# W_out's attention rows split ahead of time, mixed pairs kept on chip, v asked for later: one block of a streaming encoder in float32

## The chip, the cores and the metric

The kernel runs on one NeuronCore of a Trainium2 chip. The core has a matrix engine (TensorE, PE in the profile; its weight loads are listed apart as PEld), a vector engine (VectorE, DVE), a scalar engine (ScalarE, ACT), a general engine (GpSimd, POOL) and SyncE (SP), which here only issues DMAs. Each engine works through its own instructions in order and waits on semaphores for the others. The metric is the device time of one execution in microseconds, the median of several runs.

## The reference

One layer of a hybrid block on x of 1024 tokens by 1024 channels, all in float32. FFN width is 4096; the mixer has 8 attention heads of width 64 (512 columns, "FoX") and 512 columns of a gated linear recurrence (RG-LRU).

```python
x = layer_norm(alpha * x + 0.5 * swiglu(x, ffn1_gate, ffn1_up, ffn1_down))
z = x @ w_in                                   # q, k, v, lru x, lru gate, forget gates
fox = forgetting_attention(q, k, v, fg)        # causal softmax(q k / 8 + cum[t] - cum[s]) v
u = causal_depthwise_conv(z_lx, conv_w, conv_b)
lru = gelu(z_lg) * rg_lru(u, ...)
mix = concatenate([fox, lru], axis=-1) @ w_out
x = layer_norm(alpha * x + mix)
x = layer_norm(alpha * x + 0.5 * swiglu(x, ffn2_gate, ffn2_up, ffn2_down))
```

The first 512 rows of `w_out` meet the attention heads; they are its attention rows.

## The kernel before

**Split products.** Every float32 operand is split in two: `hi`, a rounded copy made by ScalarE (`nc.scalar.copy` into a tile of type float32r), and `lo`, the rest, made by VectorE as `x - hi`. A product is three matmuls, hi*hi + hi*lo + lo*hi (`mm3`, lines 166 to 168). A split therefore costs one ScalarE and one VectorE instruction for each tile. The big products use a scheme with seven block products in place of eight (operands "11", "21", "t1" to "t4", "22").

**Stages, in order of time.** Gate/up 1 (0 to about 640 us), down-projection 1 (to about 900), the projections of the mixer with the recurrence (`mixer_in`, to 1163), attention with W_out and the second layer norm (`attention`, 1163 to about 1380), gate/up 2 (to about 1990), down-projection 2.

**Preparation in gate/up 1.** While gate/up 1 runs on TensorE, a generator `prepare` (line 266) splits weights of later stages. Each of its steps takes a 128x256 piece of a weight that SyncE has fetched into an `aux` tile (4 buffers) and hands it to `keep` (line 280): ScalarE casts (L283), VectorE subtracts (L284), GpSimd issues a store of hi and lo to DRAM (L285). The tiles are of the pool that gate/up's own split weights use (15 buffers). `advance` (line 707) takes one step after each of the first six products of either matrix of pairs 1 to 15; what is left is done after gate/up. The jobs are, in order, the v columns of w_in (`wv_d`), the units of q, k and the recurrence (`wq_d`) and the first pair of FFN 2's gate and up (`pre_d`).

**Attention.** 64 units, one for each head h and query tile i of 128 tokens, from i = 7 down to 0; heads 6 and 7 are interleaved. `probs` makes the scores (L1389, L1390), adds the decay, and takes the maximum and the exponential (VectorE L1395, ScalarE L1396). Three units later (two from head 4 on) `to_pT` transposes the probabilities on TensorE (L1410) and splits them while evicting them (ScalarE L1414, VectorE L1415). One unit after that, for every second tile, `values` multiplies with v (L1431); for the odd head of a pair it then splits the pair's columns of the mixed result into `mixes[h // 2]` (L1443, L1444).

TensorE's gaps are filled by `piece`: the 16 products of the recurrence's mixed rows with W_out, spread over units 1 to 35. From unit 36 on there are none left. When the second head of the last pair finishes query tiles, `out_tile` multiplies all four mixed pairs with W_out's attention rows `w_fox` and adds the layer norm; the last output tiles run after the last unit, among the transposes for gate/up 2.

**W_out's attention rows.** At unit 36 `out_w` loads four row tiles of 128x1024 as two raw tiles (L1357); at units 39, 41, 43 and 45 `split_ws` splits one of them (ScalarE L158, VectorE L159).

**Where the mixed pairs live.** Pool `mixp` has two buffers. Pairs 0 and 1 are written there, stored to DRAM by GpSimd (`mix_d`, L1447) and read back by SyncE into `row` buffers at units 40 and 50 (L1532). Pair 2 is in a buffer `w2` of pool `hp`, pair 3 again in `mixp`.

**SyncE's queue.** Loads of a head (`load`, called at i = 5 of the head before, or at unit (6, 6) for head 7) bring q, kh, kl, cum (L1064, L1059) and, in the same call, v (L1374), which has two buffers. `issue_after(x)` puts what is issued inside the block behind x on its own engine's queue, with no semaphore. The rows of x for the residual (`open_row`, L1473) are in the same chain.

**Into gate/up 2.** `ready_pair` fetches the prepared weights of FFN 2's first pair from `pre_d` (L588): "11", "21" and "t1" into `ws` tiles, "t4" and "t2" into two `raw` tiles, later "t3" and "22". These fetches stand behind `mix_load`, the last read-back. The `raw` pool has two buffers for the whole kernel: in attention they hold, in turn, the last q/k unit, the fourth split row of W_out's recurrence rows (until the last `piece`), the two raw tiles of `out_w`, and then "t4" and "t2".

Of the kernel before, what the change touches and what calls it, by code (L numbers as in the profile page):

```python
# [9 lines left out]
F32 = mybir.dt.float32  # L10
F32R = mybir.dt.float32r
# [6 lines left out]
P = 128  # L18
D = 1024
T = 1024  # L20
# [28 lines left out]
def f32(ap):  # L49
    return ap.bitcast(F32)  # L50
# [12 lines left out]
class Block:  # L63
# [274 lines left out]
    def mixer_jobs(self, w_in):  # L338

        view = w_in.rearrange("(k p) f -> p k f", p=P)  # L340
        self.wq_d = self.dram.tile([len(UNITS), len(UNIT_ORDER), P, 2, 2, 2 * P], F32, name="wq_d")
        self.wv_d = self.dram.tile([2, KT, P, 2, 2 * P], F32, name="wv_d")
        jobs = []
        for cc in range(2):
            for k in range(KT):
                c = V_OFF + 256 * cc
                jobs.append(([view[:, k:k + 1, c:c + 256]], self.wv_d[cc, k]))
        for u, cols in enumerate(UNITS):
            jobs += self.quarter_jobs(view, cols, lambda n, h: self.wq_d[u, UNIT_ORDER.index(n)][:, :, h])
        return jobs  # L350
# [15 lines left out]
    def gate_up(self, wg, wu, h_d, rows, bank, tp, wsp, raws=None, later=None, aside=None, ready=None, steps=None):  # L366
# [211 lines left out]
        def ready_pair(g, u):  # L578
# [13 lines left out]
            with self.tc.issue_after(self.mix_load.ins):  # L592
                for n in ("11", "21", "t1"):
                    for m in both:
                        fetch(n, m, two_blocks())
                for n in ("t4", "t2"):
                    r = self.rawp.tile([P, 4, 4, P], F32R, tag="raw", name=self.nm("raw"))
                    for i, m in enumerate(both):
                        fetch(n, m, (r[:, 2 * i], r[:, 2 * i + 1]))
# [751 lines left out]
    def out_w(self, w_out):  # L1351

        raws = []
        for c in range(2):
            raws.append(self.raw([P, 2, D]))
            with self.tc.issue_after(self.row_load.ins):
                self.row_load = self.nc.sync.dma_start(raws[c], w_out[2 * c * P:(2 * c + 2) * P, :].rearrange("(f p) d -> p f d", p=P))  # L1357
        return [r[:, j:j + 1, :] for r in raws for j in range(2)]

    def attention(self, w_out, mixp, ln, x1_d, normed):  # L1360
# [4 lines left out]
        with self.pool("att_t", 1) as tp, self.pool("att_p", 3) as pp, self.pool("att_pt", 6) as ptp, self.pool("att_v", 2, side="right") as vtp:  # L1365

            def load(h):
                b, names = h % 2, ("q", "kh", "kl", "cum")
                if h:
                    with self.tc.issue_after(self.row_load.ins):  # L1370
                        for n in names:
                            self.load_head(h, n)
                vt = vtp.tile([P, NT, P], F32R, tag="v", name=self.nm("v"))
                self.row_load = nc.sync.dma_start(f32(vt), self.v_d[h].rearrange("(j p) d -> p j d", p=P))  # L1374
                q, kh, kl, cum = (self.heads[n][:, b, :] for n in names)
                return q, kh, kl, vt, cum
# [3 lines left out]
            def probs(h, i):  # L1380

                q, kh, kl, _, cum = heads[h]
# [39 lines left out]
            def values(h, qt):  # L1422
                vt = heads[h][3]
# [12 lines left out]
                if b:  # L1436
# [8 lines left out]
                    if qt == 0 and h < 5:  # L1445
                        for l in range(2):
                            nc.gpsimd.dma_start(mix_d[h // 2][l], f32(mixes[h // 2][l]))  # L1447

            heads, pts, ps, outs, mixes = {}, {}, {}, {}, {}
            mix_d = [self.dram.tile([2, P, T], F32, name=f"mix{c}_d") for c in range(2)]  # L1450
# [3 lines left out]
            tiles, mix, w_fox = [], [], []  # L1454
            MIXES = 40, 50
# [21 lines left out]
            with self.tc.issue_after(self.row_load.ins):  # L1477
                heads[0] = load(0)
            open_row(0)
# [6 lines left out]
            def out_tile():  # L1486
                i, d = tiles.pop(0)
                self.down_tile(i, list(zip(mix + [mixes[2], mixes[3]], w_fox)), (d,))
                if d:
                    self.layer_norm(i)  # L1490
                    normed(i)

            for n in range(len(units) + AHEAD + 1):
                if n < len(units):
                    h, i = units[n]
                    if i == 5 and h < 6 or (h, i) == (6, 6):
                        heads[h + 1] = load(h + 1)
                    if i == NT - 1:
                        if h % 2 == 0:
                            outs[h // 2] = tp.tile([P, T], F32, tag="o", name=self.nm("o"))  # L1500
                        else:
                            if h == 5:
                                t = self.hp.tile([P, 2, T], F32R, tag="w2", name=self.nm("mix"))
                                mixes[2] = t[:, 0, :], t[:, 1, :]
                            else:
                                mixes[h // 2] = tuple(mixp.tile([P, T], F32R, tag="h", name=self.nm("mix")) for _ in range(2))
# [15 lines left out]
                if n == 36:  # L1522
                    w_raws = self.out_w(w_out)
                if 39 <= n < 47 and n % 2:
                    w_fox.append(tuple(t[:, 0, :] for t in self.split_ws(w_raws[len(w_fox)], 1)))
# [3 lines left out]
                if n in MIXES:  # L1529
                    mix.append(tuple(self.rowp.tile([P, T], F32R, tag="row", name=self.nm("mix")) for _ in range(2)))  # L1530
                    for l in range(2):
                        self.mix_load = nc.sync.dma_start(f32(mix[-1][l]), mix_d[len(mix) - 1][l])  # L1532
# [6 lines left out]
def kernel(  # L1539
# [15 lines left out]
    with blk.pool("xl", side="right") as xl, blk.pool("x1") as x1, blk.pool("gu_t", 4) as tp, blk.pool("x22") as x22, \  # L1555
# [23 lines left out]
        jobs = blk.mixer_jobs(w_in[0])  # L1579
# [110 lines left out]
```

## Time and profile before

| | us |
|---|---|
| median of 3 runs | 2314.07 |
| range of the runs | 2312.58 to 2314.19 |
| the profiled execution's own time | 2308.6 |
| its span, first to last instruction | 2306.8 |
| mean granted TensorE clock | 0.998 of full speed |

The profile is of one execution. Its page lists busy time by engine, and views of its trace list busy time by stretch of time, groups of instructions by source line, who waited for whom, the chain of waits that ended last, and each engine's instructions in order. A line such as `L1415 DVE TENSOR_TENSOR pt<-a,pt` is read: line 1415, VectorE, the operation, writes tile pt from tiles a and pt. `PE a L1431 <- ACT pt L1414` means that TensorE, about to write tile a on line 1431, waited for ScalarE's writing of pt on line 1414.

### The profile page before, as it was taken

The numbers are of one execution on the slowest core, as the hardware profiler recorded it, in microseconds if no ns is written. First come the engines' busy times: TensorE is split into PE (matmuls) and PEld (weight loads), VectorE is DVE, ScalarE is ACT, GpSimd is POOL, SyncE is SP. The second block draws the span as 40 slices with busy tenths as digits, with TensorE's granted clock in tenths as the row PEclk, the third lists the DMA queues.
The fourth block names the chain that finished last, engine by engine and source line by source line (L and its number), as shares of the span: only waits on it lengthen the run. The fifth ranks groups of instructions, "written<-read, shape, count | busy, mean of one in ns | idle before, by whom it ended". The sixth has DMA issues, their size and how long they took to land.

```text
span 2306.8 us, 29448 instructions
## 1 busy us (share of the span) xinstructions
PE 2278.0 (99%) x10609; PEld 1895.0 (82%) x10609; DVE 1701.5 (74%) x2749; ACT 1063.6 (46%) x1771; POOL 308.4 (13%) x503
## 2 busy tenths in 40 slices
PE   9999999999999999999999999999999999999998
PEld 7878888888888888987788788888888888888887
DVE  8878787878467788877767899665656666577886
ACT  5454545454344335455556755333333343344341
POOL 0242323232000001121133200000000000000000
PEclk9999999999999999999999999999999999999999
DMA  4565656565376444366786734232323232564542
GB/s 155 194 212 210 211 207 216 200 223 188 108 271 221 148 142 149 131 205 203 263 249 165 246 119 151 87 119 87 119 87 119 87 119 87 201 251 159 185 144 73
DMA packets 210321, 387.10 MB, mean 168 GB/s; under 512 B 13616, under 2 KB 112240, under 8 KB 210176
## 3 DMA queue, kind: packets, MB, share of 16 engines
q1 hardware_dynamic: 173760, 262.21, 34.8%
q0 software_dynamic: 36416, 123.02, 13.6%
q8 instruction: 83, 1.36, 0.2%
q14 instruction: 62, 0.51, 0.1%
HBM read 258.27 MB, written 126.91 MB: 167 GB/s over the span
## 4 chain that ended last, share of the span: by engine, by line
PE 87%; DVE 4%; issue 4%; DMA 1%; ACT 1%; POOL 1%; SPq 0%; DVEq 0%; POOLq 0%; ACTq 0%
PE x L166 9%; PE x L168 9%; PE x L167 9%; PE b L166 7%; PE b L167 7%; PE b L168 7%; PE a L168 6%; PE a L166 6%; PE a L167 6%; PE s L168 5%; PE s L167 5%; PE s L166 5%; PE a L1431 1%; PE a L1410 1%; PE a L1093 1%
## 5 line engine op out<-in xcount | busy, mean ns | idle before, releaser
L381 ACT CAST ws<-t 128x512 fp32r<-128x512 f32 x240 | 147.7, 623 | 320.4 <-PE b L167 137.8
L382 DVE TENSOR_TENSOR ws<-t,ws 128x512 fp32r<-128x512 f32 x240 | 163.5, 685 | 71.3 <-ACT ws L381 36.2
L167 PE MATMUL a<-ws,ws 128*128 128x512 f32 x512 | 199.8, 390 | 0.6 <-DVE ws L813 0.6
L166 PE MATMUL b<-As,ws 128*128 128x512 f32 x512 | 199.7, 390 | 0.6 <-ACT As L417 0.4
L166 PE MATMUL a<-ws,ws 128*128 128x512 f32 x512 | 199.3, 390 | 0.4 <-ACT row L705 0.4
L167 PE MATMUL b<-As,ws 128*128 128x512 f32 x512 | 199.5, 390 | 0.0
L168 PE MATMUL a<-ws,ws 128*128 128x512 f32 x512 | 199.4, 390 | 0.0
L168 PE MATMUL b<-As,ws 128*128 128x512 f32 x512 | 199.3, 389 | 0.0
L166 PE MATMUL x<-As,ws 128*128 128x512 f32 x504 | 196.5, 390 | 2.8 <-ACT row L686 1.6
L168 PE MATMUL x<-As,ws 128*128 128x512 f32 x504 | 196.2, 389 | 0.0
L167 PE MATMUL x<-As,ws 128*128 128x512 f32 x504 | 196.2, 389 | 0.0
L166 PE MATMUL x<-A,ws 128*128 128x512 f32 x496 | 193.3, 390 | 0.9 <-DVE row L556 0.5
L168 PE MATMUL x<-A,ws 128*128 128x512 f32 x496 | 193.2, 389 | 0.7 <-DVE ws L382 0.7
L381 ACT CAST ws<-raw 128x512 fp32r<-128x512 f32 x180 | 110.7, 622 | 179.7 <-PE x L167 136.3
L167 PE MATMUL x<-A,ws 128*128 128x512 f32 x496 | 193.1, 389 | 0.0
L810 ACT CAST ws<-raw 128x1024 fp32r<-128x1024 f32 x112 | 117.4, 1050 | 160.9 <-PE a L167 80.9
L382 DVE TENSOR_TENSOR ws<-raw,ws 128x512 fp32r<-128x512 f32 x180 | 123.0, 686 | 91.3 <-ACT ws L381 74.3
L740 POOL DMA_DIRECT2D h_d<-row x96 | 69.5, 725 | 857.0 <-DVE row L734 840.4
L813 DVE TENSOR_TENSOR ws<-raw,ws 128x1024 fp32r<-128x1024 f32 x112 | 136.5, 1220 | 48.1 <-ACT ws L810 47.4
L166 PE MATMUL s<-ws,ws 128*128 128x512 f32 x384 | 149.5, 389 | 0.0
L168 PE MATMUL s<-ws,ws 128*128 128x512 f32 x384 | 149.5, 389 | 0.0
L167 PE MATMUL s<-ws,ws 128*128 128x512 f32 x384 | 149.5, 389 | 0.0
(354 smaller groups left out, 5408.9 us busy)
## 6 DMA issues: line engine op xcount, KB each, us to landing
raw<-h_d SPq DMA_DIRECT2D x56, 1024.0 KB, 5.5
h_d<-row POOLq DMA_DIRECT2D x96, 512.0 KB, 3.4
wd<-in_ffn_w_down_dram SPq DMA_DIRECT2D x32, 1024.0 KB, 7.6
raw<-in_ffn_w_gate_dram SPq DMA_DIRECT2D x30, 1024.0 KB, 5.2
raw<-in_ffn_w_up_dram SPq DMA_DIRECT2D x30, 1024.0 KB, 5.2
wq_d<-ws POOLq DMA_DIRECT2D x112, 256.0 KB, 3.8
wq<-wq_d SPq DMA_DIRECT2D x56, 512.0 KB, 3.6
aux<-in_w_in_dram SPq DMA_DIRECT2D x80, 128.0 KB, 3.4
```

The costliest lines, as they stand in the source:

```text
L166: mm(out, ah, bh, start=first, stop=False, skip_group_check=goes_on)
L167: mm(out, ah, bl, start=False, stop=False, skip_group_check=goes_on)
L168: self.last_mm = mm(out, al, bh, start=False, stop=last, skip_group_check=goes_on)
L381: nc.scalar.copy(hi, src)
L382: v.tensor_tensor(lo, src, f32(hi), ALU.subtract)
L740: nc.gpsimd.dma_start(d[:, 2 * n:2 * n + 2], t.rearrange("p (r t) -> p r t", r=2))
L810: cast = nc.scalar.copy(hi, src)
L813: self.mark = v.tensor_tensor(lo, src, f32(hi), ALU.subtract)
L1093: nc.tensor.matmul(pa[:, 0:width], xh, wh[:, 0:width], start=k == 0, stop=False)
L1410: nc.tensor.transpose(pa[:, (j % 4) * P:(j % 4 + 1) * P], p[:, j * P:(j + 1) * P], self.ident)
L1431: mm(pv[:, ps], vt[:, j, :], pts[h, qt][j // 4][l][:, j % 4, ps], start=j == 0 and l == 0, stop=j == last and l == 1)
```

## The change

Three things, with what follows from them.

1. `mixer_jobs` gets `w_out` as well and adds 16 jobs, one for each of the four attention row tiles and each quarter of 256 columns. They go through `keep` and leave hi and lo in a DRAM tile `wo_d`. They stand after the jobs of w_in and before those of FFN 2's first pair. In attention `out_w` and the four `split_ws` are gone; `load_out_w` reads hi and lo of one row tile from `wo_d` into two `ws` tiles, at units 30, 36, 38 and 40.
2. The mixed pairs are written where they stay: pair 0 in a `raw` tile, pair 1 in `mixp`, pair 2 in `w2` as before, pair 3 in two `row` tiles. The DRAM tiles `mix_d`, the stores and the read-backs are gone. The fetches of `ready_pair` stand behind `row_load`, the last load of the attention's chain.
3. `load` brings only q, kh, kl and cum; `load_v` brings v, at i = 2 of the head before instead of i = 5 (at unit (6, 4) instead of (6, 6) for head 7). Head 1's q and k are asked for at i = 4 instead of 5.

```diff
-    def mixer_jobs(self, w_in):
+    def mixer_jobs(self, w_in, w_out):
...
+        self.wo_d = self.dram.tile([FOX // P, 4, P, 2, 2 * P], F32, name="wo_d")
+        rows = w_out.rearrange("(f p) d -> f p d", p=P).unsqueeze(2)
         for u, cols in enumerate(UNITS):
             jobs += self.quarter_jobs(view, cols, lambda n, h: self.wq_d[u, UNIT_ORDER.index(n)][:, :, h])
+        for f in range(FOX // P):
+            for c in range(4):
+                jobs.append(([rows[f][:, :, 2 * c * P:2 * (c + 1) * P]], self.wo_d[f, c]))
         return jobs
...
-            with self.tc.issue_after(self.mix_load.ins):
+            with self.tc.issue_after(self.row_load.ins):
                 for n in ("11", "21", "t1"):
...
-    def out_w(self, w_out):
-
-        raws = []
-        for c in range(2):
-            raws.append(self.raw([P, 2, D]))
+    def load_out_w(self, f):
+
+        hi, lo = (self.wsp.tile([P, 4 * VW], F32R, tag="ws", name=self.nm("wo"))[:, 0:D] for _ in range(2))
+        for l, t in enumerate((hi, lo)):
             with self.tc.issue_after(self.row_load.ins):
-                self.row_load = self.nc.sync.dma_start(raws[c], w_out[2 * c * P:(2 * c + 2) * P, :].rearrange("(f p) d -> p f d", p=P))
-        return [r[:, j:j + 1, :] for r in raws for j in range(2)]
+                self.row_load = self.nc.sync.dma_start(f32(t).rearrange("p (c f) -> p c f", c=4), self.wo_d[f, :, :, l].rearrange("c p f -> p c f"))
+        return hi, lo
...
-                vt = vtp.tile([P, NT, P], F32R, tag="v", name=self.nm("v"))
-                self.row_load = nc.sync.dma_start(f32(vt), self.v_d[h].rearrange("(j p) d -> p j d", p=P))
-                q, kh, kl, cum = (self.heads[n][:, b, :] for n in names)
-                return q, kh, kl, vt, cum
+                return [self.heads[n][:, b, :] for n in names]
+
+            def load_v(h):
+                vts[h] = vtp.tile([P, NT, P], F32R, tag="v", name=self.nm("v"))
+                with self.tc.issue_after(self.row_load.ins):
+                    self.row_load = nc.sync.dma_start(f32(vts[h]), self.v_d[h].rearrange("(j p) d -> p j d", p=P))
...
-                    if qt == 0 and h < 5:
-                        for l in range(2):
-                            nc.gpsimd.dma_start(mix_d[h // 2][l], f32(mixes[h // 2][l]))
-
-            heads, pts, ps, outs, mixes = {}, {}, {}, {}, {}
-            mix_d = [self.dram.tile([2, P, T], F32, name=f"mix{c}_d") for c in range(2)]
+
+            heads, vts, pts, ps, outs, mixes = {}, {}, {}, {}, {}, {}
...
-            tiles, mix, w_fox = [], [], []
-            MIXES = 40, 50
+            tiles, w_fox = [], []
+            W_ROWS = 30, 36, 38, 40
...
+            load_v(0)
             open_row(0)
             open_row(1)
...
-                self.down_tile(i, list(zip(mix + [mixes[2], mixes[3]], w_fox)), (d,))
+                self.down_tile(i, list(zip([mixes[c] for c in range(4)], w_fox)), (d,))
...
-                    if i == 5 and h < 6 or (h, i) == (6, 6):
+                    if i == (5 if h else 4) and h < 6 or (h, i) == (6, 6):
                         heads[h + 1] = load(h + 1)
+                    if i == 2 and h < 6 or (h, i) == (6, 4):
+                        load_v(h + 1)
...
-                            if h == 5:
-                                t = self.hp.tile([P, 2, T], F32R, tag="w2", name=self.nm("mix"))
-                                mixes[2] = t[:, 0, :], t[:, 1, :]
+                            if h == 3:
+                                mixes[1] = tuple(mixp.tile([P, T], F32R, tag="h", name=self.nm("mix")) for _ in range(2))
+                            elif h == 7:
+                                mixes[3] = tuple(self.rowp.tile([P, T], F32R, tag="row", name=self.nm("mix")) for _ in range(2))
                             else:
-                                mixes[h // 2] = tuple(mixp.tile([P, T], F32R, tag="h", name=self.nm("mix")) for _ in range(2))
+                                t = (self.rawp if h == 1 else self.hp).tile([P, 2, T], F32R, tag="raw" if h == 1 else "w2", name=self.nm("mix"))
+                                mixes[h // 2] = t[:, 0, :], t[:, 1, :]
...
-                if n == 36:
-                    w_raws = self.out_w(w_out)
-                if 39 <= n < 47 and n % 2:
-                    w_fox.append(tuple(t[:, 0, :] for t in self.split_ws(w_raws[len(w_fox)], 1)))
+                if n in W_ROWS:
+                    w_fox.append(self.load_out_w(len(w_fox)))
...
-                if n in MIXES:
-                    mix.append(tuple(self.rowp.tile([P, T], F32R, tag="row", name=self.nm("mix")) for _ in range(2)))
-                    for l in range(2):
-                        self.mix_load = nc.sync.dma_start(f32(mix[-1][l]), mix_d[len(mix) - 1][l])
...
-        jobs = blk.mixer_jobs(w_in[0])
+        jobs = blk.mixer_jobs(w_in[0], w_out[0])
```

More of the change, by code (lines that the diff above doesn't have):

```diff
@@ L1372, in load @@
                             self.load_head(h, n)
-                vt = vtp.tile([P, NT, P], F32R, tag="v", name=self.nm("v"))
-                self.row_load = nc.sync.dma_start(f32(vt), self.v_d[h].rearrange("(j p) d -> p j d", p=P))
-                q, kh, kl, cum = (self.heads[n][:, b, :] for n in names)
-                return q, kh, kl, vt, cum
+                return [self.heads[n][:, b, :] for n in names]
[3 more added lines that the diff above has]
+                    self.row_load = nc.sync.dma_start(f32(vts[h]), self.v_d[h].rearrange("(j p) d -> p j d", p=P))
             sums, inv = self.fgz, self.wf.rearrange("p h i -> p (h i)").rearrange("p (h i) -> p h i", h=HEADS)
             def probs(h, i):
-                q, kh, kl, _, cum = heads[h]
+                q, kh, kl, cum = heads[h]
                 n = (i + 1) * P
@@ L1422, in values @@
             def values(h, qt):
-                vt = heads[h][3]
+                vt = vts[h]
                 b = h % 2
```

## The prediction

> **What bounds the kernel now.** I read the page first, then busy time by stretch, then who TensorE waits for in the one stretch that stands out, then the chain of waits through it.
>
> ```profile
> span 2306.8 us, 29448 instructions
> PE 2278.0 (99%) x10609; PEld 1895.0 (82%) x10609; DVE 1701.5 (74%) x2749; ACT 1063.6 (46%) x1771; POOL 308.4 (13%) x503
> PE 87%; DVE 4%; issue 4%; DMA 1%; ACT 1%; POOL 1%; SPq 0%; DVEq 0%; POOLq 0%; ACTq 0%
> ```
>
> TensorE (PE) is busy for 2278.0 of 2306.8 us. No part of the change adds or removes a matmul, so the change can win only from the 28.8 us in which TensorE is idle, and lose wherever it makes TensorE wait. The next rows are busy time by stretch: the columns are PE, weight loads, VectorE, ScalarE, GpSimd, clock, DMA share and GB/s.
>
> ```profile
> 520.00:580.00 60.00, 60.00 (x266) 49.69 (x266) 49.37 (x85) 28.18 (x52) 14.20 (x21) 1.00 0.52 189
> 580.00:630.00 50.00, 50.00 (x223) 41.40 (x222) 22.02 (x32) 18.48 (x29) 3.09 (x5) 1.00 0.22 75
> 1183.00:1263.00 80.00, 79.01 (x502) 70.26 (x500) 61.31 (x163) 50.78 (x125) 30.04 (x60) 1.00 0.60 167
> 1273.00:1303.00 30.00, 25.22 (x172) 21.17 (x171) 26.21 (x61) 24.61 (x58) 7.90 (x18) 1.00 0.97 300
> 1303.00:1323.00 20.00, 19.08 (x130) 16.15 (x130) 16.97 (x40) 16.42 (x38) 4.95 (x14) 1.00 0.58 210
> 1333.00:1380.00 47.00, 46.64 (x244) 38.28 (x242) 46.12 (x105) 25.20 (x51) 5.13 (x11) 1.00 0.37 135
> ```
>
> Attention runs from 1163 to 1360 us. Up to unit 35 of its 64, ready matmuls of the LRU rows (`piece`) fill TensorE's gaps: 1183 to 1263 loses 1.0 us of 80. From unit 36 there is no filler, and there the kernel splits W_out's attention rows. 1273 to 1303 loses 30.00 - 25.22 = 4.8 us, the largest loss left in the middle of the kernel. The next stretch, also without filler but with no split, loses 0.9 of 20. Who TensorE waits for between 1273 and 1303 (total, times, longest), and the split's own rows there:
>
> ```profile
> PE a L1431 <- ACT pt L1414: 1.7, 2, 1.0
> PE a L1410 <- DVE pt L1415: 1.3, 2, 0.6
> PE a L1431 <- DVE o L1441: 1.0, 1, 1.0
> L159 DVE TENSOR_TENSOR w<-raw,w 128x1024 fp32r<-128x1024 f32 x4 | 4.8, 1207 | 0.9 <-ACT w L158 0.9
> L158 ACT CAST w<-raw 128x1024 fp32r<-128x1024 f32 x4 | 4.2, 1056 | 1.3 <-DMA raw<-in_w_out_dram 1.3
> ```
>
> TensorE waits for the eviction of the transposed probabilities (L1414, L1415), and the split stands in the same two queues. The chain of waits shows one such passage whole (start, us, what):
>
> ```profile
> 1269.16 6.63 DMA raw<-in_w_out_dram
> 1275.87 1.05 ACT w L158
> 1276.95 1.23 DVE w L159
> 1278.17 0.70 DVE pt L1415
> 1278.92 1.52 PE a L1431 x11
> ```
>
> The raw rows land, ScalarE casts, VectorE subtracts, only then does VectorE evict, and TensorE's value product follows.
>
> **Part 1: the split leaves the attention.** What goes is 4 x 1.056 = 4.2 us of ScalarE, 4 x 1.207 = 4.8 us of VectorE and ScalarE's 1.3 us wait for the raw rows. What is late next is the same eviction chain without the split, and the nearest row for that is 1303 to 1323, where TensorE is busy 19.08 / 20 = 0.954 of the time. The 25.22 us of matmul at that rate take 26.4 us: a gain of 30.0 - 26.4 = **3.6 us**. Bounds: nothing, if another wait steps in, and 4.5 us at the rate of the stretch with filler (79.01 / 80: 25.5 us). I take 3.6, since the filler is used up by then. From 1333 on VectorE is busy 46.12 of 47 and TensorE 46.64 of 47; that work is unchanged and only starts earlier, so the gain passes through.
>
> A matmul's recorded busy time hides short waits, so I also take the weight loads: 21.17 us of them at 16.15 / 20 = 0.81 take 26.2 us, a gain of 3.8; at the rate with filler (70.26 / 80) 24.1 us, a gain of 5.9. [...]
>
> **Part 2: the split joins gate/up 1.** It becomes 16 steps (four row tiles by four column quarters) of `keep`, queued behind the w_in steps. Their prices (ns min/median/max, first and last start):
>
> ```profile
> L283 ACT CAST ws<-aux x156: 387/407/410, 79.5 to 578.5; 128x256 fp32r<-128x256 f32 x156
> L284 DVE TENSOR_TENSOR ws<-aux,ws x156: 413/424/428, 80.4 to 579.0; 128x256 fp32r<-128x256 f32 x156
> L285 POOL DMA_DIRECT2D pre_d<-ws x28: 667/687/989, 476.8 to 579.7; - x28
> PE x L168 <- DVE ws L382: 0.7, 1, 0.7
> PE a L166 <- ACT row L705: 0.4, 1, 0.4
> PE x L166 <- ACT row L686: 1.6, 1, 1.6
> PE x L166 <- ACT row L692: 1.1, 1, 1.1
> ```
>
> Sixteen steps are 6.5 us of ScalarE, 6.8 of VectorE and 11.0 of GpSimd issuing, with 16 loads and 16 stores. There is a place for each: 15 pairs give 15 x 12 = 180 calls of `advance`; 156 steps and the generator's opening use 157, so 173 will be used. Steps come (579.0 - 80.4) / 155 = 3.2 us apart, so the preparation ends about 51 us later, near 630. It is covered by 580 to 630, where VectorE works 22.0 of 50 us, ScalarE 18.5 and GpSimd 3.1; the stretch before, dense with steps, has VectorE at 49.4 of 60 and TensorE still at 60.00. The cover is gone if the last steps reach down-projection 1, whose first product is at 636 (the 0.4 us wait for L705 above). From 200 to 640 us TensorE lost 0.7 + 0.4 us, so 16 of 157 steps cost **0.1 us**; no row excludes the 2.7 us of the last two waits (at 162 and 169 us), which is the upper end, and nothing is the lower.
>
> **Part 3: transfers and places.** DMA issues (count, KB each, median us to landing), then what SyncE's queue waits for:
>
> ```profile
> mix_d<-mix POOLq DMA_DIRECT2D x4, 512.0 KB, 6.3
> raw<-in_w_out_dram SPq DMA_DIRECT2D x2, 1024.0 KB, 8.0
> mix<-mix_d SPq DMA_DIRECT2D x4, 512.0 KB, 9.7
> wv<-wv_d SPq DMA_DIRECT2D x4, 512.0 KB, 4.1
> v<-v_d SPq DMA_DIRECT2D x8, 512.0 KB, 3.9
> SPq L1374 <- PE a L1431: 30.7, 5, 8.3
> SPq L1357 <- PE a L168: 1.7, 1, 1.7
> SPq L588 <- DVE mix L1444: 51.0, 1, 51.0
> ```
>
> Out go 2 MB of raw rows and 2 MB of mixed pairs written and read back; in come eight loads of 512 KB (hi and lo of four row tiles) at units 30, 36, 38 and 40. The nearest load of such split weights landed in 4.1 us. The rows are first used by the output tiles, some fifteen units after the last load, so up to ten times that is covered. GpSimd loses four issues. I cost this at **0**, between -0.8 us (less traffic where the DMA share is 0.97) and +0.8. The loads at unit 36 wait for the last LRU matmul to free weight buffers, and head 5's v and head 6's q and k queue behind them; the raw loads waited there already (L1357, 1.7 us), so nothing is later.
>
> The v of head h+1 was asked for at unit 8h+2, and its load held SyncE's queue for 30.7 us in five waits until the value products of head h-1 freed the buffer. Asked for at 8h+5 it finds the buffer free. Its first use is seven units on for head 5 and five for head 7; at 2.7 us a unit (80 us, 1183 to 1263, hold some 29 units) that is 13 us or more against 3.9 to land. **0**; TensorE never waited for v, so there is nothing to win either. Head 1's q and k, one unit later in the program, stand behind the same three rows in SyncE's queue as before: 0.
>
> Pair 0 moves from GpSimd's round trip to a `raw` buffer, pair 3 to two `row` buffers; both are free long before. But pair 0 is read by the last output tile, so the `t2` weights of FFN 2, prepared in the other `raw` buffer, must wait for it. SyncE's queue and TensorE there, and how long the `ws` loads take to land:
>
> ```profile
> 1306.46 5.99 SPq L588 DMA_DIRECT2D raw<-pre_d  x8
> 1363.56 37.36 SPq L588 DMA_DIRECT2D ws<-pre_d  x20
> 1378.98 0.39 PE L168 MATMUL a<-w,mix 128*128 128x512 f32 x1
> 1380.20 0.47 PE L166 MATMUL x<-A,ws 128*128 128x512 f32 x1 [0.39 <-issue]
> DMA to landing us min/median/max: 2.5/3.9/8.4
> ```
>
> Four of the eight `raw` loads move from 1306 to after 1379. `t2` is the ninth product of the pair; eight products of twelve matmuls, at 50 us for 223 (580 to 630), are 21.5 us, so it is due near 1402, and loads issued at 1379 to 1383 with 8.4 us to land come some 10 us ahead. Behind them wait `t3`, `22` and the next raw weights, which waited for TensorE before as well. **0**, unless the order is the third rival's.
>
> **Sum:** -3.6 + 0.1 + 0 = -3.5 us on the profiled execution (2308.6 us, 1.8 of it around the span). The median of the runs shown is 2314.07, 5.5 us above for a reason that the profile doesn't show; I apply the difference to the median: **2310.6**. What a measurement can tell from no change here is about 0.2%, 4.6 us.
>
> **Rivals.** (1) *The stall only moves.* ScalarE is busy 24.6 of 30 us and VectorE 26.2; without the split TensorE may still wait for L1414 and L1441 in the order in which the queues happen to stand. For it: 1303 to 1323 still loses 0.9 us. Against it: most of the listed waits follow a split instruction at once. Gain 0 to 1, so 2313.6. Chance 0.16.
>
> (2) *TensorE gets the rate it has with filler.* Gain 4.5 to 5.9, say 5.2: 2308.9. For it: hidden waits go too. Against it: no filler is there. Chance 0.2. [...]
>
> (3) *SyncE's queue is blocked by `t2`.* If its four loads stand ahead of the `ws` loads, those start not at 1363.6 but after the last output tile at 1379.4, with four issues (3 us) and 8.4 us to land before them: the first product comes at 1390.8 instead of 1380.2, 10.6 us late. Net +7.0: 2321. It decides as soon as one `t2` load precedes the first `ws` load. For it: the `raw` loads do go first now. Against it: they did so because their buffers came free earlier, and now `t2`'s comes free last. Chance 0.1.
>
> (4) *The change doesn't do what it says* (the split still in attention, or a round trip left): the edits leave no such line; under 0.01.
>
> **How the numbers follow.** Forecast 0.53, rivals 0.16, 0.2, 0.1, 0.01. Faster by over 0.2% holds most of rival 2 and the top of the forecast's spread: 0.22. Slower by over 0.2% is rival 3 less its milder forms: 0.09. Within: 0.69. The range reaches from 5.9 + 0.8 us and the runs' own 0.8 below the median (2306.6) to no gain with the 2.7 us of part 2 above it (2316.8).
>
> **What would show it.** Right: no cast or subtract of W_out after 1163 us; 1273 to about 1299 with TensorE busy over 0.94; 172 `keep` casts in gate/up 1, the last before 632; no `mix_d`; first product of FFN 2 within 1 us of the last output tile. Wrong: TensorE losing 4 us between 1273 and 1303 again (rival 1), a gap of some us before FFN 2's first product (rival 3), a wait near 636 (part 2), or value products waiting for v.

## The result and the profile after

| | before | after |
|---|---|---|
| median of 9 runs each, taken side by side (us) | 2310.84 | 2305.57 |
| range (us) | 2307.90 to 2314.19 | 2302.63 to 2307.26 |
| ratio, 95% interval | | 0.9975 [0.9966, 0.9983] |
| the same, measured again | | 0.9979 [0.9970, 0.9988] |
| span of the profiled execution (us) | 2306.8 | 2301.9 |

The change makes the kernel 0.2 to 0.25% faster: 4.9 to 5.8 us by the ratios, 4.9 by the spans. The forecast was 2310.6, so it was 5.0 us too high. Of these, 3.2 are the reference, which measured 2310.84 here in place of 2314.07 (the three runs shown were among the four slowest of these nine); the other 1.8 are the forecast's own. The measured time lies 1.0 us below the forecast's range, which began at 2306.6.

The page of the kernel after begins:

```profile
span 2301.9 us, 29566 instructions
PE 2278.3 (99%) x10609; PEld 1894.2 (82%) x10609; DVE 1702.2 (74%) x2761; ACT 1063.8 (46%) x1783; POOL 313.3 (14%) x515
```

TensorE is busy as long as before (2278.0), so over the whole span the gain is idle time, 23.6 us in place of 28.8. Busy time by stretch of the kernel after, for the two stretches on which the prediction rested (PE, weight loads, VectorE, ScalarE, GpSimd, clock, DMA share, GB/s):

```profile
1273.00:1303.00 30.00, 28.81 (x201) 24.40 (x199) 25.56 (x69) 24.51 (x64) 7.62 (x21) 1.00 0.96 264
1303.00:1323.00 20.00, 19.64 (x124) 16.55 (x125) 16.21 (x35) 13.48 (x31) 3.78 (x11) 1.00 0.33 122
```

The stretch that lost 4.8 us loses 1.2. VectorE and ScalarE are as busy in it as before (26.21 and 24.61): with the split gone, they do other work there sooner. What TensorE still waits for in all of attention, 1163 to 1420 us:

```profile
PE s L1395 <- DVE m L1401: 3.2, 6, 1.8
PE a L1416 <- DVE pt L1421: 0.4, 2, 0.2
PE s L1396 <- DMA kl<-k_d: 0.3, 1, 0.3
PE a L1437 <- DVE pt L1421: 0.2, 1, 0.2
```

The longest wait for evicted probabilities is now 0.2 us (1.0 before). What is left is scores that wait for the maximum of an earlier unit; 1.8 us of it is one wait in attention's first units, outside the stretch of the change.

**A common measure.** Fixed stretches catch other work as soon as two kernels drift apart. So I follow TensorE from the first score product of unit 36 (the filler is used up) to that of unit 48 and to the first product of FFN 2. From unit 36 to FFN 2 every version does the same matmuls (some 610), except e10, which has 13 more there. Up to unit 48 the count differs with the order (159 before, 144 after), so the parts are compared by their idle time. Busy time by stretch with these bounds, before, then after:

```profile
1271.22:1298.57 27.35, 22.63 (x159) 19.14 (x158) 23.56 (x55) 21.88 (x51) 7.12 (x16) 1.00 0.97 317
1271.22:1380.20 108.98, 102.71 (x610) 85.61 (x609) 98.94 (x227) 71.44 (x156) 19.31 (x46) 1.00 0.55 186
```

```profile
1271.62:1292.16 20.54, 20.02 (x144) 17.44 (x142) 17.35 (x46) 16.11 (x42) 3.33 (x12) 1.00 1.02 296
1271.62:1374.98 103.36, 101.67 (x610) 85.33 (x609) 93.95 (x222) 66.68 (x151) 16.85 (x44) 1.00 0.54 170
```

From unit 36 to FFN 2 the kernel takes 103.36 in place of 108.98 us, 5.6 less (104.00 in a second profile: 5.0 less). Idle time fell by 6.27 - 1.69 = 4.6, of which 4.2 in units 36 to 48 (4.72 to 0.52); the other 1.0 sits inside the recorded busy time of the same 610 matmuls.

### The profile page after: what moved, and what is told of

It reads as the page before. It is cut to its first block, busy times and chain, and to the rows that moved or that the text cites. A ratio compares the mean times of both kernels' runs of the same rounds, so it can differ in the third digit from the quotient of the medians.

```text
span 2301.9 us, 29566 instructions
## 1 busy us (share of the span) xinstructions
PE 2278.3 (99%) x10609; PEld 1894.2 (82%) x10609; DVE 1702.2 (74%) x2761; ACT 1063.8 (46%) x1783; POOL 313.3 (14%) x515
## 4 chain that ended last, share of the span: by engine, by line
PE 83%; issue 6%; DVE 5%; DMA 2%; POOL 2%; ACT 1%; SPq 0%; DVEq 0%; POOLq 0%; ACTq 0%
PE x L168 8%; PE x L166 8%; PE x L167 8%; PE b L166 6%; PE b L167 6%; PE b L168 6%; PE a L168 6%; PE a L166 6%; PE a L167 6%; PE s L168 5%; PE s L167 5%; PE s L166 5%; PE a L1437 1%; PE a L1416 1%; PE a L1098 1%
```

## The experiments

All runs below are timed beside the kernel before. The last column is the stretch from unit 36 to FFN 2 of the one profiled execution, read as above.

| run | median us | ratio to before | unit 36 to FFN 2 |
|---|---|---|---|
| before | 2310.1 to 2311.3 | 1 | 108.98 |
| after / again | 2305.57 / 2306.12 | 0.9975 / 0.9979 [0.9970, 0.9988] | 103.36 / 104.00 |
| e1_split_only | 2309.30 | 0.9993 [0.9984, 1.0001] | 106.30 |
| e2_split_back | 2305.54 | 0.9979 [0.9969, 0.9989] | 105.35 |
| e4_v_early | 2306.62 | 0.9982 [0.9973, 0.9990] | 103.57 |
| e5_fine_loads | 2310.82 | 1.0002 [0.9994, 1.0011] | 110.15 |
| e6_dummy_reads | 2308.62 | 0.9989 [0.9980, 0.9998] | 106.14 |
| e7_unused_steps | 2312.81 | 1.0007 [0.9998, 1.0016] | 109.01 |
| e8_split_time_back | 2306.39 | 0.9985 [0.9976, 0.9993] | 104.89 |
| e9_rest_on_gpsimd | 2305.97 | 0.9984 [0.9975, 0.9993] | 103.39 |
| e10_read_back_early | 2316.54 | 1.0029 [1.0017, 1.0041] | 118.87 |
| e11_split_back_early | 2311.23 | 1.0001 [0.9992, 1.0010] | 110.87 |
| e12_dummy_reads_early | 2304.87 | 0.9975 [0.9966, 0.9983] | 103.31 |
| e13_read_back_late | 2311.97 | 1.0003 [0.9995, 1.0012] | 110.88 |
| e14_steps_last | 2305.46 | 0.9980 [0.9971, 0.9989] | 103.37 |
| e15_reads_order_of_after | 2306.60 | 0.9981 [0.9972, 0.9990] | 103.47 |
| e16_after_order_of_reads | 2309.07 | 0.9990 [0.9982, 0.9999] | 105.78 |
| e17_before_order_of_e2 | 2312.65 | 1.0003 [0.9994, 1.0012] | 111.22 |
| e18_e2_order_of_before | 2309.09 | 0.9990 [0.9981, 0.9999] | 107.30 |

### Which part makes the gain

Theory: the split's queue time leaving attention (the prediction). Rival: the pairs' places or the late v. e1 makes the first part of the change alone. e2 takes it back alone, but loads W_out's rows raw as four transfers of 512 KB into `row` tiles, where the kernel before has two of 1 MB into `raw` tiles. e4 asks for v early again.

```diff
--- before, e1 (mix_d, the pairs' places and load() as before)
+        for f in range(FOX // P):
+            for c in range(4):
+                jobs.append(([rows[f][:, :, 2 * c * P:2 * (c + 1) * P]], self.wo_d[f, c]))
...
-                if n == 36:
-                    w_raws = self.out_w(w_out)
...
+                if n in W_ROWS:
+                    w_fox.append(self.load_out_w(len(w_fox)))
--- after, e2 (the 16 jobs of the steps are gone as well)
+        raws = [self.row() for _ in range(4)]
...
-                if n in W_ROWS:
-                    w_fox.append(self.load_out_w(len(w_fox)))
+                if n == 36:
+                    w_raws = self.out_w(w_out)
+                if 39 <= n < 47 and n % 2:
+                    w_fox.append(tuple(t[:, 0, :] for t in self.split_ws(w_raws[len(w_fox)], 1)))
--- after, e4
-                    if i == (5 if h else 4) and h < 6 or (h, i) == (6, 6):
+                    if i == 5 and h < 6 or (h, i) == (6, 6):
                         heads[h + 1] = load(h + 1)
-                    if i == 2 and h < 6 or (h, i) == (6, 4):
+                    if i == 5 and h < 6 or (h, i) == (6, 6):
                         load_v(h + 1)
```

> The kernel before with only the preparation of W_out's attention rows moved to gate/up 1 (loads at units 30, 36, 38, 40); mixed pairs still go through DRAM, v is still asked for early. Queue theory (all of the gain in attention is the four casts and four subtractions leaving the queues of ScalarE and VectorE): TensorE idle between 1263 and 1420 us falls from 6.3 to 1.7 us, as in the changed kernel, and the time is 4 to 5.5 us below before (ratio about 0.998). Transfer theory (the part of the gain above my 3.6 us comes from the round trip and v): idle there stays near 2.7 us, about 1 us worse than the changed kernel. Cost of the 16 steps in gate/up 1 by both: under 0.6 us.

> The changed kernel with only its first part undone: the rows are loaded raw into four row buffers at unit 36 and split at units 39, 41, 43 and 45, as before; pairs in their final places and the late v stay. Queue theory: idle between 1263 and 1420 us returns to about 6 us, the time to that of before within 1 us. Transfer theory: idle about 5.3 us, 1 us better than before.

> The changed kernel with v asked for at i = 5 again (and head 1's q and k too). Both theories of the split say no difference: idle between 1263 and 1420 us 1.7 us within 0.4. If v's place in SyncE's queue matters, the value products wait for v, or idle grows by more than 0.5 us.

> The changed kernel once more beside the others: the same idle by stretch within 0.2 us between 1183 and 1420, with only the first 40 us (landing of the first rows of x) free to differ by about 1 us. Ratio 0.9975 within 0.001.

The theory fell. With the split gone and the round trip left (e1) 1.6 us are won, which the interval (-0.2 to 3.7) doesn't part from nothing; with the split left in attention and the round trip gone (e2) it is 4.9, as much as the whole change. The late v is worth nothing (e4). In e1 the stall moved: units 36 to 48, then 48 to 63 of e1, with the second row of the kernel after below it:

```profile
1275.83:1297.09 21.26, 20.15 (x144) 17.44 (x142) 18.10 (x48) 16.85 (x45) 4.79 (x15) 1.00 1.04 332
1297.09:1350.47 53.38, 50.05 (x303) 42.46 (x304) 45.31 (x105) 36.14 (x79) 9.84 (x26) 1.00 0.51 168
```

```profile
1292.16:1343.48 51.32, 50.23 (x304) 42.14 (x304) 45.68 (x107) 36.59 (x83) 10.57 (x27) 1.00 0.36 115
```

Units 36 to 48 are almost as quick as after, and units 48 to 63 lose 2.1 us more (1.4 against the second profile).

### What the split and its new steps cost

e5 makes e2's finer raw loads alone. e7 adds the 16 steps to the kernel before, unused. e8 gives the kernel after the split's queue time back (a copy of each hi tile onto itself on ScalarE, and on VectorE). e9 and e14 move the steps' work.

```diff
--- before, e5 (each load in its issue_after block, as before)
-                self.row_load = self.nc.sync.dma_start(raws[c], w_out[2 * c * P:(2 * c + 2) * P, :].rearrange("(f p) d -> p f d", p=P))
+            for j in range(2):
+                f = 2 * c + j
+                self.row_load = self.nc.sync.dma_start(raws[c][:, j, :], w_out[f * P:(f + 1) * P, :])
--- before, e7 (with the jobs' loops as in the kernel after)
+                jobs.append(([rows[f][:, :, 2 * c * P:2 * (c + 1) * P]], self.wo_d[f, c]))
--- after, e8
+                if 39 <= n < 47 and n % 2:
+                    hi, lo = w_fox[(n - 39) // 2]
+                    for _ in range(1):
+                        nc.scalar.copy(hi, f32(hi))
+                    for _ in range(1):
+                        v.tensor_tensor(hi, f32(hi), f32(hi), ALU.max)
--- after, e9 (eng is GpSimd for the 16 steps)
-            v.tensor_tensor(lo, src, f32(hi), ALU.subtract)
+            eng.tensor_tensor(lo, src, f32(hi), ALU.subtract)
--- after, e14 (wo_jobs: the 16 jobs, no longer in mixer_jobs)
...
+        jobs += blk.wo_jobs
         steps = blk.prepare(jobs, wsp, ap)
```

> The kernel before with W_out's raw rows loaded as four transfers of 512 KB in place of two of 1 MB, everything else as before. The version with the pairs in place and the split left in attention (2305.5 against 2310.2 us) also had these smaller loads. If they made its gain (ScalarE waits 1.1 us for such a load in the kernel before): about 2306 to 2307.5 us. If the places of the pairs made it: 2310 us, within 1 us of the kernel before.

> The kernel before with the 16 added keep steps in gate/up 1 whose result nobody reads; attention as before. The prediction: 0.1 us, so 2310.2 to 2310.4 us. By the landmarks of the runs so far (matmuls 2200 to 2400 and 2600 to 2650 take 0.9 to 2.3 us longer in every version with these steps): 2311 to 2312.5 us.

> The kernel after with one idle copy of each of W_out's four row tiles on ScalarE and one on VectorE (128x1024, values unchanged) at units 39, 41, 43 and 45: the queue time of the split without its loads. If the queue time of the split is what costs in the kernel before (the prediction's Part 1, 3.6 us): 2309 to 2310 us. If it costs only what the version with the split left in attention lost from unit 36 on (1.3 to 2.0 us): 2307 to 2308 us.

> The kernel after with the remainders of W_out's 16 keep steps (128x256) subtracted on GpSimd in place of VectorE. If the price of these steps (about 1 to 2 us upstream of attention, with a TensorE wait of 0.57 us near 595 us for a VectorE result) comes from VectorE's queue: the wait near 595 goes, and the time is 1 to 2 us under the kernel after, 2304 to 2305 us. If it comes from their transfers or ScalarE's casts: 2305.5 to 2306.5 us, no change.

> The kernel after with W_out's 16 keep steps behind the FFN2 ones in gate/up 1, not ahead of them. If their price depends on which steps meet VectorE's fullest stretch: matmuls 2600 to 2650 take 11.3 us again in place of 12.2, and the time is 2304.5 to 2305.5 us. If it is only the count of steps that matters: 2305.5 to 2306.5 us, as the kernel after.

The finer loads alone win nothing (e5; why is told further on). The split's queue time, put back without its loads, costs 1.5 us from unit 36 on in the profile (104.89 against 103.36; 0.9 against 104.00), and 0.3 to 0.8 us between the medians, inside their intervals: far from 3.6. By its trace e8 also runs its attention in another order than the kernel after, so even this isn't the queue time by itself. The steps cost 0.0007 of 2310, 1.6 us, with an interval from -0.5 to 3.7. TensorE's waits from 480 to 640 us in e7, and in e14:

```profile
PE x L168 <- DVE ws L387: 0.8, 1, 0.8
PE a L166 <- ACT row L710: 0.5, 1, 0.5
```

```profile
PE a L166 <- ACT ws L813: 0.9, 1, 0.9
```

The first row, near 595 us, is new against the kernel before; the 50 matmuls around it take 12.4 in place of 11.3 us, worked out from their starts. Behind the other steps (e14) it goes, and a wait of 0.9 us appears at the start of down-projection 1. With the steps' subtract on GpSimd (e9) the wait goes as well, the same 50 matmuls take 11.6, and matmuls at 500 to 546 us take 0.7 longer. By the matmuls' starts the price is about 1 us in all three places; the medians of e9 and e14 don't part from the kernel after.

### Is it the round trip's transfers?

New theory: with the round trip the DMA engines are full in units 36 to 56 (a share of 0.97 in units 36 to 48 of the kernel before), and rows of W_out and of heads 6 and 7 land late. e6 adds four copies of 512 KB to the kernel after where the read-back was; e12 adds them earlier. e10 and e13 move the kernel before's first read-back, and e11 moves e2's loads and splits.

```diff
--- after, e6 (e12: n in (20, 28))
+                if n in (40, 50):
+                    for _ in range(2):
+                        with self.tc.issue_after(self.row_load.ins):
+                            moved.append(nc.sync.dma_start(far[len(moved)], x1_d[len(moved) * P:(len(moved) + 1) * P, :]))
--- before, e10 (e13: 46, 50)
-            MIXES = 40, 50
+            MIXES = 26, 50
--- e2, e11
-                if n == 36:
+                if n == 29:
                     w_raws = self.out_w(w_out)
-                if 39 <= n < 47 and n % 2:
+                if n in (32, 36, 38, 41):
```

> The kernel after with four added copies of 512 KB from DRAM to DRAM on SyncE's queue at units 40 and 50, where the kernel before reads its two pairs back; nothing waits for them. If the round trip costs by its transfers (DMA engines full, head 6's rows late, PE late in units 48 to 56): as with the split moved alone, 2308 to 2309.5 us, DMA share over 1.0 from 1283 to 1313 and 2 to 3 us of idle PE in units 48 to 56. If it costs by what else hangs on it (GpSimd's stores, SyncE's waits, the tiles' places): 2305.5 to 2306.5 us, like the kernel after.

> The kernel after with the same four added copies of 512 KB from DRAM to DRAM, now at units 20 and 28 in place of 40 and 50, where they cost 2.5 to 3 us. If such traffic costs only where the DMA engines are full already: 2305.5 to 2306.5 us, like the kernel after. If it costs wherever it is (SyncE's issue, rows of the next head held up): 2308 to 2309 us again.

> The kernel before with the first pair read back at unit 26 in place of 40, where the DMA engines are busy 0.5 to 0.75; the second stays at 50. If the round trip costs because its transfers fall into a full stretch (units 40 to 56): the idle time of TensorE in units 40 to 48 (4.6 us) falls to 2 us or less, and the time to about 2307.5 us. If it costs by the split's queue time or by the round trip's stores and waits wherever they are: 2309.5 to 2310.5 us.

> The version with the pairs in place and W_out split in attention from four raw loads (2305.5 us), with the loads at unit 29 and the splits at units 32, 36, 38 and 41 in place of 39 to 45, so that the first falls into the stretch where VectorE and ScalarE have time (4.5 to 8.4 of 10 us). It has no added steps in gate/up 1. If the split's queue time in units 36 to 48 still costs the 1 to 2 us that this version loses there: 2304 to 2305 us. If what is left isn't the split's: 2305.5 us as before.

> The kernel before with the first pair read back at unit 46 in place of 40, behind the raw rows and head 6's rows; nothing else differs (the stores, the buffers and the split are as before). If the loss of the kernel before in units 40 to 48 is made by these two transfers, which land among W_out's raw rows and ahead of head 6's q, k and cum: the second raw load lands about 3 us earlier, the idle time there falls from 4.6 to under 2 us, and the time to 2306 to 2308 us. If it is made by the split's queue time, or by the round trip's stores: 2309.5 to 2310.5 us.

e6 and e12 came out as the transfers' theory has it. e13 did not: the read-back stood behind the raw rows and head 6's, and nothing was won. But the raw rows landed no earlier in it: the second raw load landed 10.1 us after unit 36 began, in the kernel before 9.6. The other half of the round trip was still beside them: GpSimd issues its two stores of pair 1, 512 KB each, at 1270.8 and 1271.4 in the kernel before and at 1272.0 and 1272.5 in e13. So e13 speaks against the read-back, and not against the round trip as a whole. e10 and e11 told nothing of the question, because in both a load that waited for its buffer held SyncE's queue: in e10 a load of v (L1374), ahead of the second half of the read-back, in e11 the first raw row of W_out. What SyncE's queue waited for in e10, then in e11:

```profile
SPq L1374 <- PE a L1431: 36.8, 3, 22.8
```

```profile
SPq L1356 <- PE a L168: 23.5, 1, 23.5
```

While one load waits 23 us for a buffer nothing behind it is issued, and the next head's q and k are requested 15 us late (1271 in place of 1256 us).

### Transfers or order

In these runs each engine took its instructions in the order that the built program holds (the starts in e15 to e18 below stand in the orders given to them; in e17 these move 92 TensorE, 57 VectorE and 35 ScalarE instructions), and that order is set by the scheduler that builds the program. Compared instruction by instruction, the built programs show what e6 had changed beside the traffic, with four copies that nothing waits for: 72 TensorE, 29 VectorE and 19 ScalarE positions, all in units 48 to 57. e12 has the kernel after's order on all three engines, e4 too but for six rows, and e13 has that of the kernel before. So every run that kept an order had kept its time, within the intervals of the ratios. The last four hold the transfers and exchange the orders, by edges that only fix the order of issue:

```diff
--- e15 = e6 in after's order; e16 = after in e6's; e17 = before in e2's; e18 = e2 in before's
+    for order in ORDERS:
+        names = [f"I-{n}" for n in order if f"I-{n}" in by]
+        for a, b in zip(names, names[1:]):
+            tc.add_manual_dep(by[b], a, mb.DependencyInfo(mb.DependencyClass.NoSync, mb.DependencyReason.DATA), reason="order")
```

> The kernel with the four added copies on SyncE's queue at units 40 and 50 (2308.6 us), with edges that make TensorE, VectorE and ScalarE stand in the kernel after's order: the scheduler that builds the program had placed 72 TensorE, 29 VectorE and 19 ScalarE instructions of attention otherwise once the copies were there. If the order costs, and not the transfers: 2305.5 to 2306.5 us, as the kernel after, and units 48 to 56 take 18 us in place of 22.7. If the transfers cost on the chip: 2308 to 2309 us.

> The kernel after, without any added copy, with edges that give the three engines the order of the kernel with the copies. If the order costs: 2308 to 2309 us, with units 48 to 56 at 22 to 23 us in place of 18. If the transfers cost: 2305.5 to 2306.5 us.

> The kernel before, round trip, raw loads and split all there, with edges that give TensorE, VectorE and ScalarE the order of the version with the pairs in place and the split left (2305.5 us); 92 TensorE, 57 VectorE and 35 ScalarE instructions of attention stand otherwise, the four splits among them. If the order is what the places of the pairs changed: 2305.5 to 2307 us. If it is the round trip on the chip (late raw rows, full DMA engines): 2309.5 us or more, since splits that stand earlier then wait longer for their raw rows.

> The version with the pairs in place and the split left in attention (2305.5 us), with the kernel before's order on the three engines and no round trip. If the order costs: 2309.5 to 2311 us, with about 4.5 us of idle TensorE in units 40 to 48. If the round trip costs on the chip: 2305.5 to 2306.5 us.

Units 48 to 63 of e6, e15 and e16:

```profile
1294.44:1348.55 54.11, 50.48 (x305) 42.43 (x304) 46.13 (x107) 36.66 (x83) 10.60 (x27) 1.00 0.42 136
```

```profile
1296.61:1348.01 51.40, 50.28 (x304) 42.22 (x304) 45.70 (x107) 36.66 (x83) 10.55 (x27) 1.00 0.42 138
```

```profile
1297.70:1351.41 53.71, 50.54 (x305) 42.41 (x304) 46.07 (x107) 36.76 (x83) 10.59 (x27) 1.00 0.35 109
```

e15 moves e6's bytes in the kernel after's 51.3 us; e16 moves none of them and takes e6's longer time, within 0.4 us. The medians agree (2306.60 and 2309.07). So here the order accounts for the time; the bytes by themselves cost nothing that these runs can tell. The stall that moved in e1 is probably order too: the starts in its trace match e6's order better than the kernel after's (8 TensorE rows out of line from unit 36 on, against 39). No run exchanged it. One place where it shows, VectorE's first `p` of 1024 columns of head 7 in the timelines of after and of e16:

```profile
1306.06 1.22 DVE L1401 CUSTOM_DVE_ANT_0 p<-s,cum 128x1024 f32<-128x1024 f32 x1
```

```profile
1314.17 1.23 DVE L1401 CUSTOM_DVE_ANT_0 p<-s,cum 128x1024 f32<-128x1024 f32 x1
```

That is 13.9 us after unit 48 began (1292.16), and 16.5 (1297.70): head 7's first scores stand further back in TensorE's queue, and its first exponential comes 2.6 us later.

For the kernel before it is both, as far as one profile of each run and the ratios tell. e18, its order without the round trip, units 36 to 48:

```profile
1273.37:1299.32 25.95, 22.43 (x160) 19.20 (x158) 23.29 (x55) 21.75 (x51) 7.33 (x14) 1.00 0.86 254
```

3.5 of the 4.7 us of idle time remain when the round trip is gone. e2, with the same work in its own order, has 23.29 - 21.11 = 2.2, though it leaves 17 of the matmuls for later. To unit 63, where these counts nearly meet again, the idle time is 5.8 us before, 4.6 in e18 and 2.7 in e2. Units 36 to 48 of e2:

```profile
1271.74:1295.03 23.29, 21.11 (x143) 17.56 (x142) 21.65 (x50) 19.99 (x46) 4.54 (x13) 1.00 0.83 263
```

e17 has that order and the round trip, and doesn't win: its splits stand earlier, but the second raw load lands 9.5 us after unit 36 began, as late as in the kernel before, where e18's last lands after 6.1. Units 36 to 48 of e17, ScalarE's wait ahead of the cast in it, and TensorE's waits from 1273 to 1302:

```profile
1273.61:1301.81 28.20, 23.12 (x144) 19.94 (x142) 21.96 (x50) 20.02 (x46) 5.33 (x15) 0.88 0.92 304
```

```profile
  DMA raw<-in_w_out_dram: 2.9, 1
```

```profile
PE a L1410 <- DVE pt L1415: 3.0, 1, 3.0
PE a L1431 <- DVE pt L1415: 0.9, 1, 0.9
PE a L1410 <- ACT p L1396: 0.9, 1, 0.9
```

It takes 4.9 us more than e2: 2.9 of idle time, about the one wait of 3.0 behind late rows, and 2.0 of busy time at a lower granted clock (0.88; the last section shows where). So the better order pays only where the rows land in time.

e5 belongs here. The finer loads alone also set the units in another order, with the four splits closer together, and e5 is as slow as the kernel before. Its units 36 to 48:

```profile
1271.74:1298.73 26.99, 21.64 (x144) 18.74 (x142) 21.84 (x51) 20.46 (x46) 5.37 (x15) 0.94 0.92 302
```

Its last raw load lands 10.8 us after unit 36 began (9.6 in the kernel before), so the smaller loads did not bring the rows earlier beside the round trip. But e5 can't tell whether e2 owes its order to the finer loads, to the places of the pairs or to the absent transfers.

From unit 36 to FFN 2, in profiles: round trip out with the order held, 108.98 to 107.30, -1.7 (v later and the raw loads finer with it, which weren't tried in this order alone); e2's own order, to 105.35, -1.9; the split out as well, to 103.36 or 104.00, -1.4 to -2.0; then about +1 in gate/up 1. By medians, e18 stands between before and e2 as well, with intervals that overlap e2's.

## Why the prediction was wrong

- **What bounds the kernel**: right in the place. Of the 5.6 us from unit 36 on, 4.2 are idle time of TensorE in units 36 to 48, where the prediction located it, and 0.4 idle time behind them. That the change can win only from idle time didn't hold in this stretch: 1.0 us came out of the recorded busy time of the same matmuls.
- **Part 1, 3.6 us**: the failed step is "most of the listed waits follow a split instruction at once". They do, but the order in which the units stand is worth as much (1.9 us, e18 to e2) as taking the split out (1.4 to 2.0, e2 to the kernel after). The split out of attention alone (e1) saved 2.7 us from unit 36 on, about 1.7 after the steps' price, which fits its ratio (1.6); its queue time put back (e8) cost 0.9 to 1.5. Rival 1, the stall that moves, describes e1: 1.4 to 2.1 us of it came back in units 48 to 63.
- **Part 2, 0.1 us**: mis-sized, within its bounds (0 to 2.7). It measured about 1 us by the matmuls' starts and 1.6 [-0.5, 3.7] by the ratio. VectorE had time on average (busy 22.02 of 50 us from 580 to 630 in the kernel before), but from 590 to 602 us it is busy 9.70 of 12 us (7.73 before), and one subtract of gate/up's own came 0.6 us late there. The end of the preparation was right: near 630 predicted, and in the kernel after

```profile
L284 DVE TENSOR_TENSOR ws<-aux,ws x172: 411/423/428, 80.7 to 623.1; 128x256 fp32r<-128x256 f32 x172
```

- **Part 3, transfers and places at 0, between -0.8 and +0.8**: the main failure. It measured 3.6 us from unit 36 on (before to e2). Two things were left out. First, the round trip delays what is waited for: W_out's raw rows land 9.6 us after unit 36 began, beside two of the stores of mixed pairs, and 6.1 without the round trip; with the order held, its end is worth 1.7 us (e18). Second, the program was taken as the old one with rows removed; but with other loads and places the scheduler set the units in another order, worth 1.9 us. The late v at 0 was right (e4).
- **Rivals**: `t2` did not block (rival 3): its loads were issued at 1372.7, behind the first twelve `ws` loads (1358.9), and FFN 2's first product followed the last output product within 0.7 us. Rival 2 gave attention's size, 5.2, by a cause that isn't the one found. That a matmul's recorded busy time hides short waits held: in the kernel before matmuls of 128x512 are recorded at 0.39 us with starts 0.23 us apart (1298.89, 1299.12, 1299.35), and 1.0 of the 5.6 us was hidden inside the recorded time of the same 610 matmuls (102.71 to 101.67).
- **The sum**: -3.5 against -4.9 to -5.8. Two errors of opposite sign (the split's gain credited too high, the round trip's at nothing) left it 1.4 to 2.3 short, so that it came as near as it did is in part luck. It was put on a median that later runs of the same kernel, 2310.1 to 2311.3, don't repeat.
- **Its signs**: all that it listed for being right came true (no split after 1163 us, TensorE busy 28.81 of 30 us between 1273 and 1303, 172 casts, no `mix_d`, no gap before FFN 2), because none of them tells the split's gain from the round trip's.

**What stays open.** No version tried is measurably faster than the kernel after (e2, e12 and e14 lie within 0.7 us of it). Why one order is better, beyond the place shown, wasn't taken apart further, nor which edit of e2 made the scheduler choose its order. TensorE's first score product varies from 1163.9 to 1169.7 us between profiles; before it ScalarE waits 3.5 to 5.5 us for a store of k in five profiles that were compared. Whether the steps have a part in that isn't settled. The 5.5 us between the profiled execution and the shown median of before were not explained.

## What to carry to other kernels

Where a scheduler sets the order, an edit isn't the old program minus some rows: compare the two programs' orders before giving a time difference to the traffic or the work that was edited, and test it by holding one and exchanging the other. A wait that follows a long instruction in an in-order queue doesn't show that the instruction is the cause; put its length back elsewhere and see. Signs named beforehand should differ between the rivals. And a median of three runs can be 3 us off one of nine, more than half of what this change is worth.

## What the runs showed of the hardware

**TensorE was busy with the DMA engines full.** In the kernel after TensorE is busy 20.02 of the 20.54 us of units 36 to 48 at a DMA share of 1.02. In e15, with added copies, the same units take 20.56 us at 1.06. In e6 the copies cost only through the order (units 48 to 63 take 54.11 us, and 51.40 with the same copies in the kernel after's order); in e17, where rows of W_out are waited for (2.9 us by ScalarE, 3.0 by TensorE behind it), landing late did cost.

**The granted clock fell to half after a stall of TensorE.** Stretches of e17 around its wait of 3.0 us:

```profile
1278.00:1281.00 3.00, 0.09 (x1) 0.09 (x2) 1.71 (x3) 2.76 (x6) 0.00 (x0) 1.00 1.01 401
1283.00:1285.00 2.00, 1.51 (x7) 1.51 (x8) 2.00 (x8) 2.00 (x5) 0.29 (x1) 0.50 1.03 420
1285.00:1287.00 2.00, 2.00 (x11) 1.90 (x11) 2.00 (x3) 1.66 (x5) 0.00 (x0) 0.50 1.07 248
1287.00:1289.00 2.00, 2.00 (x7) 1.60 (x6) 1.45 (x4) 0.43 (x2) 0.00 (x0) 0.50 1.04 260
```

The granted clock is 0.50 for six us from 1283 on, two us after the wait ended (0.96 in between, 0.84 from 1289 to 1291). So the 3.0 us of the wait are not all that e17 loses there: the busy time of units 36 to 48 is 2.0 us longer than e2's as well (23.12 us for 144 matmuls, 21.11 for 143). In e13 no gap of TensorE from 1272 on was over 1.61 us (what the first stretch below is idle), and in the last the clock is 0.59:

```profile
1282.00:1284.50 2.50, 0.89 (x6) 0.48 (x4) 2.14 (x5) 1.97 (x4) 0.29 (x1) 1.00 1.03 246
1288.00:1292.00 4.00, 2.74 (x19) 1.89 (x17) 3.50 (x8) 3.95 (x8) 1.93 (x3) 1.00 0.97 316
1292.00:1296.00 4.00, 3.81 (x17) 3.41 (x17) 3.31 (x9) 2.65 (x7) 0.59 (x2) 0.59 0.97 382
```

What makes the clock fall these runs don't tell; the same kernel showed it in one execution and not in another (after, 1163 to 1183 us: 1.00 in the first profile, 0.91 in the second). By an estimate from these rows, four us at 0.59 lose 4 x 0.41 = 1.6 us, most of the 1.9 us by which e13, in the kernel before's order, is longer from unit 36 on (110.88 against 108.98).
